# A convolution tile held ahead of a layer norm, gate columns moved behind it, ones products in the next norm's wait, and four more weights' low parts by VectorE

## Chip, cores and metric

One core of a Trainium2 chip runs the whole kernel. The metric is the device time of one execution in microseconds (us), as the median of several runs. "The profile" is one execution recorded by the hardware profiler, with its page and its trace.

## What is computed

A decoder trunk of two layers over 1024 tokens (S) of 1024 channels (D), float32 in and out. Cut to what matters:

```python
for i in range(2):
    mod = silu(c) @ ada_w[i] + ada_b[i]            # six vectors of D per layer
    sh_m, sc_m, g_m, sh_f, sc_f, g_f = split(mod, 6)
    h = rms_norm(x, norm_mix_g[i]) * (1 + sc_m) + sh_m
    if i == 0:                                     # convolution mixer
        a, g = split(h @ w1 + b1, 2)
        u = a * sigmoid(g)
        u = causal_depthwise_conv(u, w_dw, 31 taps) + b_dw
        y = silu(layer_norm(u)) @ w2 + b2
    else:                                          # pooling mixer, windows 2, 4, 8, 16
        y = grouped(trailing_mean(h) - h) @ w_grp * ls
    x = x + (1 + g_m) * y
    h = rms_norm(x, norm_ffn_g[i]) * (1 + sc_f) + sh_f
    x = x + (1 + g_f) * ((silu(h @ w_gate) * (h @ w_up)) @ w_down)   # inner width 2816
out = rms_norm(x, final_g)
```

The vector g_f of layer 0 is the "output gate" of the title: modulation j = 5, first used where the first feed-forward block's down products are added to x.

## The kernel before

**Layout.** Channels lie on the 128 partitions, in KT = 8 tiles of 128; tokens lie along the free dimension, in two halves, A (tokens 0 to 511) and B (512 to 1023). The halves go through the same stages one after the other, so that one half's products can stand in PE's queue while the other half's elementwise work is done. A is ahead of B.

**Weights in two parts.** A product in full float32 is made of three fast ones: high part of the weight with high part of the activation, high with low, low with high. So a product of one 128-channel tile of weights is 3 x 8 = 24 instructions ("24 products"). A weight of 128x1024 arrives in a `raw` buffer by a DMA that SP issues; ACT copies the rounded high part into a `w` tile; the low part comes in one of two ways. Either ACT writes the negated high-order copy of raw and POOL issues a DMA that reads the weight a second time and adds it (`load_weight(summed=True)`, line 413), or DVE subtracts (`low=V_`; a unit marked `own` takes this way, lines 546 and 564). There are nine `w` tiles (`W_BUFS`), so a weight's loading waits for products that free the tiles of an earlier one.

**Order.** PE's order is written by hand: `unit(...)` appends a piece of work to a list, and `run_units` emits them one after another, with the weights that they take loaded ahead. `need(name)` puts all that is left of a task there. Tasks are generators of elementwise work (norms, taps of the convolution, layer norm); `pace` steps them between PE's units by a planner's clock of what each engine has been given. A task that yields a word waits until a planned time: those in `LOAD` are counted from PE's clock, "stats" from the work given to DVE and ACT. The order on the other engines is then a scheduler's.

**The stage of the change** (layer 0, convolution):

- `conv_in((B, p))` makes the 24 + 24 products of a and g for B's tile p. A's layer norm (`layer_norm_silu`, task `ln_a`) needs A's eight tiles of convolved u; its sum `acc` is spread over the partitions by `mean`, a product with ones, and the variance by `var` and `rstd`. `rest` is B's tiles 0 to 4. With `HOLD = 1` the last of them (p = 4, the "held tile") is emitted behind the output products `y` of A (`conv_out(A)`); `HOLD_LN` is the number of tiles that stand just ahead of `need("ln_a")`. The steps of `ln_a` on PE (`mean`, `var`, `rstd`) fall among the tiles' products where the planner's clock puts them.
- `ada_columns` works out modulations j = 2 to 5 of layer 0 on PE, as products of columns of `ccols` with rows of the weight (`ada<-adaw`), two weights to a group; two buffers (`ADA_BUFS`) hold the weights, which SP loads. `columns_done` spreads the result (`adac`), and DVE adds the bias. All four modulations are done before `y` of A, but for the spread of the last, which stands behind `y`'s first three outputs.
- The norm that follows `conv_out(A)` (`norm`, task `norm_a`, through `mean_rsqrt`) takes the sum of squares of x (`var`), a root on DVE (`col`), its spreading (`rstd`), and gives the eight tiles of h as `hhi` and `hlo` to the feed-forward's `gate` and `up` products. `need("norm_a")` ends it.
- Behind it start the modulation of layer 1 (`ada_task(1, ...)`, dots on DVE), B's taps and B's layer norm, beside A's feed-forward. `conv_out(B)` stands `OUT_B = 3` units before that block's end.
- From B's feed-forward of layer 0 on, `ffn_mixed` emits a block: plain pairs, then pairs made with fewer products out of sums of quarters, and `rest`, the plain units from f = 16 to 21, in which one unit (`rest[4]`) has its weights' low parts by DVE and the other units of down products `dn` (`ffn_p2`) theirs by POOL's DMAs.

`warm(count)` emits products of ones with ones, whose result nobody reads (tile `idle`); before, it is used only at the kernel's start.

Of the kernel before, what the change touches and what calls it, by code (L numbers as in the profile page):

```python
# [39 lines left out]
HOLD = 1  # L40
FIRST = 4
SHARED = (5, 6)
HOLD_LN = 0
# [6 lines left out]
LOAD = {"load": 6.0, "late": 15.0, "settle": 8.0, "slow": 18.0, "next": 4.0}  # L50
# [63 lines left out]
def trunk(ctx, tc, xT, c, vec, ada, adan, w1, w2, wgu, wdn, wpl, wph, out):  # L114
# [94 lines left out]
    class Task:  # L209
# [6 lines left out]
        def step(self, e):  # L216
            if e != "V" or self.done or clock["PE"] < self.until and not forced[0]:
                return False
            try:
                if self.mark is None:  # L220
                    self.mark = clock["PE"] - V_.spent
                said = next(self.gen)
                if said == "wait":
                    return False
                if said in LOAD:
                    self.until = clock["PE"] + LOAD[said]
                elif said is not None:
                    self.until = (self.mark + V_.spent if self.urgent else max(clock["V"], clock["S"])) + (DELAY if self.urgent or not lax[0] else DELAY_BEHIND)[said]
                    self.mark = None
            except StopIteration:  # L230
                self.done = True
                tasks.remove(self)
            return True
# [206 lines left out]
    def mean_rsqrt(acc, n, keep=False, tag="col1"):  # L440

        count = n // P
        yield "stats"
        b = bank("var")
        for i in range(count):
            matmul(b[:, i : i + 1], acc[:, i * P : (i + 1) * P], ones[:, 0:1], start=True, stop=True)
        v, t = b[:, :count], b[:, 16 : 16 + count]  # L450
        V_.tensor_scalar(v, v, EPS, None, op0=ADD)
        col = tmp.tile([P, 16], F32, tag=tag, name=nm("col"), bufs=1)[:, :count]
        yield from rsqrt(v, col, t)
        yield "spread"
        r = spare_bank("rstd") if "taps_done" in st else bank("rstd")
        for i in range(count):
            matmul(r[:, i * P : (i + 1) * P], col[:, i : i + 1].broadcast_to([P, P]), ident, start=True, stop=True)
        r = r[:, :n]
        if not keep:
            return r  # L460
        held = temp(n, "ny", 2)
        S_.copy(held, r)
        return held
# [58 lines left out]
    def norm(ch, l, ffn, key, keep=False, squares=None):  # L522
        h = [(slot(ch, "hhi"), slot(ch, "hlo")) for _ in range(KT)]
        st[key] = h
        if squares is not None:
            rstd = yield from mean_rsqrt(squares.acc, ch.n, keep)
# [261 lines left out]
    def layer_norm_silu(ch):  # L788
# [9 lines left out]
        yield "stats"  # L798
# [26 lines left out]
    def conv_out(ch, squares, then=None):  # L825
# [20 lines left out]
        for ds in [(0, 1, 2), *((d,) for d in range(3, KT))]:  # L846
# [343 lines left out]
    def ffn_mixed(ch, l, until, at_end=False):  # L1190
# [25 lines left out]
        if not at_end:  # L1216
            rest[4] = own(rest[4])
# [76 lines left out]
    idle = spare_bank("idle")  # L1294

    def warm(count):
        for _ in range(count):
            matmul(idle[:, :P], ones, ones, start=True, stop=True)

# [140 lines left out]
    def ada_first(take):  # L1440
        T["ada", 0] = Task(ada_columns((2, 3, 4, 5)), False, 0)
        T["ada", 0].free = True
# [27 lines left out]
    conv_out(A, sq_a, lambda take: [now(columns_done(*g, bank("adac"))) for g in held_back])  # L1470
    unit(lambda take: T.__setitem__("norm_a", Task(norm(A, 0, True, ("h", 0), squares=sq_a), True)))
    for p in rest[len(rest) - HOLD :]:
        conv_in((B, p))
    need("norm_a")
    unit(lambda take: stretch.__setitem__(0, STRETCH))


    unit(lambda take: T.__setitem__(("ada", 1), ada_task(1, range(6))))
# [3 lines left out]
    for i, (e, ws) in enumerate(fa):  # L1482
        if i == len(fa) - OUT_B:
# [3 lines left out]
            unit(lambda take: T.__setitem__("norm_bf", Task(norm(B, 0, True, ("h", 1), squares=sq_b), True)))  # L1487
        unit(e, *ws)
    need("norm_bf")
# [122 lines left out]
```

## Time and profile before

| what | value |
|---|---|
| median of three runs | 1824.46 us |
| the three runs | 1816.51 to 1829.71 us |
| the profiled execution | 1815.78 us |
| its span in the trace | 1814.0 us |
| its mean granted TensorE clock | 0.993 |
| PE busy | 1774.6 us, 98% |
| DVE / ACT / POOL busy | 1317.4 / 1028.3 / 568.6 us |
| DMA | 335.39 MB, mean 185 GB/s |

The span is what the trace covers from first to last instruction; the execution's own time is 1.8 us more. A row of a timeline gives the start, the time of the row's instructions together, engine, line, operation, out<-in by the program's tile names, shapes and count, and in brackets the idle time ahead of it with what ended it. A float32 product that is not in the fast form leaves two records: four `ada` instructions are x8, ten `idle` are x20.

### The profile page before, as it was taken

To read this page: it belongs to the slowest core of one execution; us is meant where nothing else is said; L and a number is where in the kernel's file an instruction comes from. 1 tells how busy PE (TensorE), PEld (TensorE's weight loads), DVE (VectorE), ACT (ScalarE), POOL (GpSimd) and SP (SyncE) were. 2 spreads that over 40 slices of the span, in tenths; PEclk is the share of its full clock that TensorE was granted. 3 is DMA by queue.
4 is the path that set the end of the run, shared out by engine and by line. 5 is a ranking of instruction groups with operands and counts; after the bars stand their busy time and mean duration, and the time that the engine had idled before them with its cause. 6 is when DMAs were issued, how large, how long until landed. Compare 5 with 4: busy or idle time off the path is not lost.

```text
span 1814.0 us, 26209 instructions
## 1 busy us (share of the span) xinstructions
PE 1774.6 (98%) x9748; PEld 1518.4 (84%) x9748; DVE 1317.4 (73%) x2133; ACT 1028.3 (57%) x1597; POOL 568.6 (31%) x620
## 2 busy tenths in 40 slices
PE   9999899999999999999999999999999999999997
PEld 7777677888888788899998878999987889999986
DVE  8689846988774228889978468787694578887745
ACT  4776667767656455555554456555544546555543
POOL 0389724877833112111117122111161211011111
PEclk9999999999999999999999999999999999999998
DMA  9868767888978887867766877545558866655462
GB/s 308 278 183 258 190 165 192 223 219 227 233 190 219 231 217 192 242 198 209 205 155 144 203 165 184 142 130 136 134 139 196 185 138 169 180 140 140 125 142 70
DMA packets 113937, 335.39 MB, mean 185 GB/s; under 512 B 11281, under 2 KB 21649, under 8 KB 113810
## 3 DMA queue, kind: packets, MB, share of 16 engines
q1 hardware_dynamic: 76656, 222.56, 36.5%
q0 software_dynamic: 36000, 110.12, 34.0%
q8 instruction: 76, 1.25, 0.3%
q10 hardware_dynamic: 1154, 1.05, 0.2%
q14 instruction: 51, 0.42, 0.1%
HBM read 329.49 MB, written 4.19 MB: 184 GB/s over the span
## 4 chain that ended last, share of the span: by engine, by line
PE 83%; DMA 4%; DVE 4%; issue 4%; POOL 3%; ACT 2%; POOLq 0%; SPq 0%; DVEq 0%; ACTq 0%
PE dn L130 23%; PE gate L130 23%; PE up L130 22%; PE y L130 4%; PE a L130 3%; PE first L130 2%; DMA w<-in_wdn_dram 2%; PE g L130 2%; DMA adaw<-in_adan_dram 1%; ACT w L108 1%; POOL pa L108 1%; DMA w<-in_w_dram 1%; PE ada L130 1%; POOL w L413 1%; DVE t L108 1%
## 5 line engine op out<-in xcount | busy, mean ns | idle before, releaser
L130 PE MATMUL dn<-ghi,w 128*128 128x512 f32 (+1 forms) x1440 | 469.6, 389 | 5.7 <-DMA w<-in_wdn_dram 5.2
L108 ACT CAST w<-raw 128x1024 fp32r<-128x1024 f32 (+1 forms) x390 | 319.8, 823 | 154.6 <-PE dn L130 66.9
L108 ACT ACTIVATE w<-raw 128x1024 fp32r<-128x1024 f32 (+1 forms) x250 | 230.4, 921 | 304.0 <-PE dn L130 100.7
L108 DVE SCALAR_TENSOR_TENSOR x<-dn,gains,x 128x512 f32<-128x512 f32 (+1 forms) x360 | 263.1, 736 | 86.1 <-PE dn L130 82.9
L130 PEld LDWEIGHTS dn<-ghi,w 128*128 128x128 f32 x1440 | 269.1, 189 | 59.8 <-DMA w<-in_wdn_dram 7.0
L130 PE MATMUL gate<-hhi,w 128*128 128x512 f32 (+1 forms) x1088 | 310.3, 358 | 0.0
L130 PE MATMUL up<-hhi,w 128*128 128x512 f32 (+1 forms) x1088 | 310.1, 358 | 0.0
L130 PE MATMUL dn<-glo,w 128*128 128x512 f32 (+1 forms) x720 | 279.4, 388 | 0.1
L108 POOL TENSOR_TENSOR pa<-pa,pr 128x512 f32<-128x512 f32 x170 | 234.8, 1489 | 23.1 <-ACT pr L108 20.5
L1064 POOL DMA_DIRECT2D w<-in_wgu_dram x80 | 69.7, 871 | 499.4 <-PE up L130 147.5
L130 PEld LDWEIGHTS gate<-hhi,w 128*128 128x128 f32 x1088 | 196.7, 189 | 30.9
L130 PEld LDWEIGHTS up<-hhi,w 128*128 128x128 f32 x1088 | 196.6, 189 | 30.5
L130 PE MATMUL gate<-hlo,w 128*128 128x512 f32 (+1 forms) x544 | 195.0, 358 | 1.4 <-DVE hlo L108 1.4
L130 PE MATMUL up<-hlo,w 128*128 128x512 f32 (+1 forms) x544 | 194.6, 358 | 0.0
L413 POOL DMA_DIRECT2D w<-in_wgu_dram x92 | 82.2, 893 | 312.8 <-ACT w L108 289.1
L108 DVE SCALAR_TENSOR_TENSOR ca<-u,vecs,ca 128x512 f32<-128x512 f32 x250 | 174.0, 750 | 0.9
L108 DVE TENSOR_TENSOR t<-t,up 128x512 f32<-128x512 f32 (+1 forms) x88 | 54.9, 625 | 154.7 <-PE up L130 134.6
L130 PEld LDWEIGHTS dn<-glo,w 128*128 128x128 f32 x720 | 136.1, 189 | 23.3 <-POOL glo L108 0.5
L108 DVE TENSOR_TENSOR w<-raw,w 128x512 fp32r<-128x512 f32 (+1 forms) x140 | 107.7, 775 | 33.0 <-ACT w L108 29.7
L108 ACT ACTIVATE pr<-u,vecs 128x512 f32<-128x512 f32 x170 | 115.3, 717 | 24.1 <-POOL pa L108 16.9
L130 PEld LDWEIGHTS gate<-hlo,w 128*128 128x128 f32 x544 | 102.6, 189 | 17.9 <-DVE hlo L108 2.3
L130 PEld LDWEIGHTS up<-hlo,w 128*128 128x128 f32 x544 | 102.7, 189 | 15.5
(193 smaller groups left out, 3333.8 us busy)
## 6 DMA issues: line engine op xcount, KB each, us to landing
raw<-in_wgu_dram SPq DMA_DIRECT2D x176, 512.0 KB, 5.0
w<-in_wgu_dram POOLq DMA_DIRECT2D x92, 512.0 KB, 8.0
raw<-in_wdn_dram SPq DMA_DIRECT2D x88, 512.0 KB, 5.4
adaw<-in_ada_dram SPq DMA_DIRECT2D x64, 512.0 KB, 5.2
raw<-in_w_dram SPq DMA_DIRECT2D x42, 512.0 KB, 6.4
w<-in_wdn_dram POOLq DMA_DIRECT2D x42, 512.0 KB, 8.3
w<-in_wgu_dram POOLq DMA_DIRECT2D x80, 256.0 KB, 5.4
adaw<-in_adan_dram SPq DMA_DIRECT2D x32, 512.0 KB, 6.0
```

The source lines that it names most:

```text
L108: self.last = self.order(getattr(self.eng, name)(out, *args, **kw))
L130: last_mm[0] = nc.tensor.matmul(out, lhsT, rhs, start=start, stop=stop, **kw).ins.name
L413: order(nc.gpsimd.dma_start(as_src(lo), src, accum_op=ADD))
L1064: order(nc.gpsimd.dma_start(lo, src, accum_op=ADD))
```

## The change

It has five parts.

1. The held tile goes from behind `y` of A to ahead of it (`HOLD` 0, `HOLD_LN` 1). The layer norm's steps shift against the tiles: `mean` from behind tile 2 to the middle of tile 3, `var` and `rstd` from tile 3's g to tile 4's. A's `mean` is timed from PE's clock ("mean": 6.0) rather than from DVE's.
2. The output gate's columns (j = 5) are a generator of their own, `gates`. The spread of j = 4 stays behind the first unit of `conv_out(A)`, and there the generator issues its first two loads; its four groups of products come behind `conv_out(A)`, behind `need("norm_a")`, and behind the first two units of A's feed-forward; the spread and the start of layer 1's modulation come at unit `GROUP + 1` = 3.
3. `mean_rsqrt` of `norm_a` gets ten ones products behind `var` and ten behind `rstd`.
4. `conv_out(B)` begins with a unit of two outputs, not three.
5. In `ffn_mixed`, two units of down products (f = 16, 17 and f = 20, 21) get their weights' low parts by DVE: four weights in each of two blocks. Eight accumulating DMAs of POOL and eight negated copies of ACT go, eight subtractions of 128x1024 on DVE come.

The diff, without what repeats:

```diff
-HOLD = 1
+HOLD = 0
 FIRST = 4
 SHARED = (5, 6)
-HOLD_LN = 0
+HOLD_LN = 1
...
-LOAD = {"load": 6.0, "late": 15.0, "settle": 8.0, "slow": 18.0, "next": 4.0}
+LOAD = {"load": 6.0, "late": 15.0, "settle": 8.0, "mean": 6.0, "slow": 18.0, "next": 4.0}
...
                 if said in LOAD:
                     self.until = clock["PE"] + LOAD[said]
+                    if said == "mean":
+                        self.mark = None
...
+    def warm(count):
+        if count:
+            idle = spare_bank("idle")
+            for _ in range(count):
+                matmul(idle[:, :P], ones, ones, start=True, stop=True)
+
-    def mean_rsqrt(acc, n, keep=False, tag="col1"):
+    def mean_rsqrt(acc, n, keep=False, tag="col1", warmed=0):
...
             matmul(b[:, i : i + 1], acc[:, i * P : (i + 1) * P], ones[:, 0:1], start=True, stop=True)
+        warm(warmed)
         v, t = b[:, :count], b[:, 16 : 16 + count]
...
             matmul(r[:, i * P : (i + 1) * P], col[:, i : i + 1].broadcast_to([P, P]), ident, start=True, stop=True)
+        warm(warmed)
...
     def layer_norm_silu(ch):
...
-        yield "stats"
+        yield "stats" if ch.i else "mean"
         b = bank("mean")
...
     def conv_out(ch, squares, then=None):
...
-        for ds in [(0, 1, 2), *((d,) for d in range(3, KT))]:
+        n = 2 if ch.i else 3
+        for ds in [range(n), *((d,) for d in range(n, KT))]:
...
     def ffn_mixed(ch, l, until, at_end=False):
...
         if not at_end:
-            rest[4] = own(rest[4])
+            for i in (4, 5, -1):
+                rest[i] = own(rest[i])
...
     def ada_first(take):
-        T["ada", 0] = Task(ada_columns((2, 3, 4, 5)), False, 0)
+        T["ada", 0] = Task(ada_columns((2, 3, 4)), False, 0)
...
     sq_a = Squares(A)
-    conv_out(A, sq_a, lambda take: [now(columns_done(*g, bank("adac"))) for g in held_back])
-    unit(lambda take: T.__setitem__("norm_a", Task(norm(A, 0, True, ("h", 0), squares=sq_a), True)))
+    gates = ada_columns((5,))
+
+    def spread_held(take):
+        now(columns_done(*held_back.pop(), bank("adac")))
+
+    def gates_ahead(take):
+        spread_held(take)
+        next(gates)
+    conv_out(A, sq_a, gates_ahead)
+    unit(lambda take: next(gates))
+    unit(lambda take: T.__setitem__("norm_a", Task(norm(A, 0, True, ("h", 0), squares=sq_a, warmed=10), True)))
     for p in rest[len(rest) - HOLD :]:
         conv_in((B, p))
     need("norm_a")
+    unit(lambda take: next(gates))
     unit(lambda take: stretch.__setitem__(0, STRETCH))
-    unit(lambda take: T.__setitem__(("ada", 1), ada_task(1, range(6))))
     taps(B, *range(KT))
     put("ln_b", lambda: layer_norm_silu(B))
     fa = ffn(A, 0, False)
...
+        if i == GROUP + 1:
+            unit(spread_held)
+            unit(lambda take: T.__setitem__(("ada", 1), ada_task(1, range(6))))
         unit(e, *ws)
+        if i < GROUP:
+            unit(lambda take: next(gates, None))
```


**Order on PE at A's mean.** Before, g of B's tile 2 ends (`g_1990`), the mean follows, then a group of ada and a of tile 3 (`a_2126`):

```order
L130 MATMUL g_1990<-hhi_777,w_1834 128x512
L130 MATMUL g_1990<-hlo_778,w_1834 128x512
L130 MATMUL g_1990<-hhi_777,w_1835 128x512
L130 MATMUL mean_2064<-acc_1622,ones 128x512
L130 MATMUL ada_2003<-adaw_2014,ccols 32x256 x4
L130 MATMUL ada_2003<-adaw_2016,ccols 32x256 x4
L130 MATMUL a_2126<-hhi_763,w_1954 128x512
L130 MATMUL a_2126<-hlo_764,w_1954 128x512
L130 MATMUL a_2126<-hhi_763,w_1955 128x512
```

With the change, tile 2's products are followed by a of tile 3 (`a_2059`), then the mean and g of tile 3 (`g_2060`):

```order
L130 MATMUL a_2059<-hlo_778,w_1952 128x512
L130 MATMUL a_2059<-hhi_777,w_1953 128x512
L130 MATMUL a_2059<-hhi_779,w_1952 128x512
L130 MATMUL a_2059<-hlo_780,w_1952 128x512
L130 MATMUL a_2059<-hhi_779,w_1953 128x512
L130 MATMUL mean_2092<-acc_1624,ones 128x512
L130 MATMUL g_2060<-hhi_765,w_1980 128x512
L130 MATMUL g_2060<-hlo_766,w_1980 128x512
L130 MATMUL g_2060<-hhi_765,w_1981 128x512
```

Tile 3's 24 products of a moved from behind the mean to ahead of it, and the ada groups behind it are gone.

**Order on PE behind the output products of A.** Before, the last `y` is followed by a of the held tile:

```order
L130 MATMUL y_2573<-vhi_2234,w_2454 128x512
L130 MATMUL y_2573<-vlo_2235,w_2454 128x512
L130 MATMUL y_2573<-vhi_2234,w_2455 128x512
L130 MATMUL a_2629<-hhi_763,w_2492 128x512
L130 MATMUL a_2629<-hlo_764,w_2492 128x512
L130 MATMUL a_2629<-hhi_763,w_2493 128x512
```

and 24 rows further by the norm's `var`, with g of the held tile behind it:

```order
L130 MATMUL a_2629<-hhi_777,w_2492 128x512
L130 MATMUL a_2629<-hlo_778,w_2492 128x512
L130 MATMUL a_2629<-hhi_777,w_2493 128x512
L130 MATMUL var_2655<-ones,acc_2381 128x1 x4
L130 MATMUL g_2630<-hhi_763,w_2530 128x512
L130 MATMUL g_2630<-hlo_764,w_2530 128x512
L130 MATMUL g_2630<-hhi_763,w_2531 128x512
```

With the change, a group of ada stands behind `y`, then `var`, ones, `rstd`, ones, a group of ada and the feed-forward's gate products:

```order
L130 MATMUL y_2593<-vlo_2248,w_2474 128x512
L130 MATMUL y_2593<-vhi_2247,w_2475 128x512
L130 MATMUL ada_2631<-adaw_2423,ccols 32x256 x4
L130 MATMUL ada_2631<-adaw_2425,ccols 32x256 x4
L130 MATMUL var_2660<-ones,acc_2396 128x1 x4
L130 MATMUL idle_2665<-ones 128x128 x10
L130 MATMUL rstd_2689<-ident,col_2677 128x128 x4
L130 MATMUL idle_2694<-ones 128x128 x10
L130 MATMUL ada_2631<-adaw_2640,ccols 32x256 x4
L130 MATMUL ada_2631<-adaw_2642,ccols 32x256 x4
L130 MATMUL gate_2757<-hhi_2644,w_2512 128x512
L130 MATMUL gate_2757<-hlo_2645,w_2512 128x512
```

Forty-eight products of the held tile left this place; two groups of ada and twenty ones products came.

**The down group's low parts in layer 0, B, beside the pool mixer of A.** Before, POOL's row has two accumulating DMAs for them between the mixer's windows (`win`):

```order
L108 TENSOR_TENSOR win_9148<-win_9148,recip 128x15
L108 TENSOR_TENSOR win_9177<-win_9176 128x524
L108 TENSOR_TENSOR win_9148<-win_9148,hp_8876 128x15
L108 TENSOR_TENSOR win_9177<-win_9176 128x512
L413 DMA w_9261<-in_wdn_dram 128x1024
L108 TENSOR_TENSOR win_9177<-win_9177,recip 128x15
L108 TENSOR_TENSOR win_9177<-win_9177,hp_8877 128x15
L413 DMA w_9270<-in_wdn_dram 128x1024
L413 DMA w_9332<-in_wpl_dram 128x1024
L413 DMA w_9339<-in_wpl_dram 128x1024
```

With the change, DVE's row has the subtractions (`w_9294`, `w_9302`) between the same mixer's steps:

```order
L108 TENSOR_TENSOR mxlo_9169<-win_9144,mxhi_9168 128x512
L108 SCALAR_TENSOR_TENSOR win_9189<-win_9189,hp_8909 128x497
L108 TENSOR_TENSOR w_9294<-raw_9291,w_9293 128x1024
L108 CAST mxhi_9205<-win_9189 128x512
L108 TENSOR_TENSOR mxlo_9206<-win_9189,mxhi_9205 128x512
L108 TENSOR_TENSOR win_9247<-win_9248 128x520
L108 TENSOR_TENSOR w_9302<-raw_9299,w_9301 128x1024
L108 SCALAR_TENSOR_TENSOR win_9248<-win_9248,hp_8910 128x497
L108 TENSOR_TENSOR t_9286<-t_9286,up_9215 128x512
L108 CAST mxhi_9256<-win_9248 128x512
```

The two low parts left POOL's queue and stand between DVE's steps of the mixer (`mxhi`, `mxlo`).

More of the change, by code (lines that the diff above doesn't have):

```diff
@@ L520, in modulated, with norm @@
         V_.scalar_tensor_tensor(lo, t, sh, hi.bitcast(F32), op0=ADD, op1=SUB)
-    def norm(ch, l, ffn, key, keep=False, squares=None):
+    def norm(ch, l, ffn, key, keep=False, squares=None, warmed=0):
         h = [(slot(ch, "hhi"), slot(ch, "hlo")) for _ in range(KT)]
@@ L525, in norm @@
         if squares is not None:
-            rstd = yield from mean_rsqrt(squares.acc, ch.n, keep)
+            rstd = yield from mean_rsqrt(squares.acc, ch.n, keep, warmed=warmed)
         else:
@@ L1293, in trunk @@
         matmul(spread_c[h], ones[0:1, :], crow[:, h * 512 : h * 512 + 512], start=True, stop=True)
[L1294 to L1298, printed above, removed]
     acc = temp(A.n, "acc", 2)
```

## The prediction

> **What bounds the kernel now.** The page's first part says that TensorE is busy almost throughout, so only its gaps and its clock can be won. The waits of PE, largest first, name them:
>
> ```profile
> PE 1774.6 (98%) x9748; PEld 1518.4 (84%) x9748; DVE 1317.4 (73%) x2133; ACT 1028.3 (57%) x1597; POOL 568.6 (31%) x620
> PE mean L130 <- DVE mod L108: 7.0, 1, 7.0
> PE dn L130 <- DMA w<-in_wdn_dram: 5.2, 4, 1.9
> PE ada L130 <- DMA adaw<-in_adan_dram: 4.2, 3, 2.6
> PE y L130 <- DMA w<-in_w_dram: 2.2, 3, 1.3
> ```
>
> Columns: who waits for what, us in total, times, longest. These four are 18.6 us, 1.0% of the run, and the edits touch the order at each. The busy time per stretch has the granted clock third from the end of a row:
>
> ```profile
> 207.00:215.00 8.00, 0.98 (x3) 0.50 (x2) 5.42 (x9) 2.49 (x4) 4.40 (x6) 0.74 0.90 183
> 215.00:232.00 17.00, 17.00 (x98) 11.79 (x96) 10.56 (x25) 10.37 (x15) 4.08 (x4) 0.92 0.53 149
> 232.00:238.00 6.00, 3.23 (x20) 1.24 (x19) 3.01 (x5) 2.63 (x5) 0.87 (x1) 0.73 0.95 257
> 1366.00:1379.00 13.00, 12.22 (x46) 9.87 (x47) 6.29 (x9) 1.38 (x3) 0.00 (x0) 0.87 0.53 129
> ```
>
> Behind a gap of some 2 us the clock falls as well, and that costs about as much as a short gap: 6.0 x (1 - 0.73) = 1.6 us at 232, 13.0 x (1 - 0.87) = 1.7 at 1366.
>
> **The mean of A's layer norm.** Between PE's last `pz`, which ends at 194.29, and the mean stand two runs of 24 products today (a and g of B's tile 2) with a group of ada between; with the change it is three runs of 24 (a and g of tile 2, then a of tile 3) and no ada: the held tile, 4, takes the later place beside `var` and `rstd` that tile 3 had. The first two rows below are of the timeline and of the chain of work that ended last, the next two of that chain, the last of the timeline:
>
> ```profile
> 194.29 0.50 PE L130 MATMUL a<-hhi,w 128*128 128x512 f32 x1
> 282.90 5.44 PE a L130 x24
> 209.85 1.30 POOL pa L108
> 213.49 0.69 DVE acc L108
> 214.33 2.05 PE L130 MATMUL mean<-acc,ones 128*128 128x512 f32 x2 [7.02 <-DVE mod L108]
> ```
>
> PE would reach the mean at 194.29 + 3 x 5.44 = 210.6. The sum that it reads ends at 213.49 + 0.69 = 214.18, behind a chain of POOL's adds for the last tap and two DVE adds, whose places on their engines the change leaves as they are. The wait is then 214.2 - 210.6 = 3.6 instead of 7.02: **-3.4**. POOL's and DVE's rows in that stretch get one instruction more or less of 0.7 to 1.3, so I leave the chain 2 us on either side: -5.4 to -1.4. The clock falls behind 3.6 as it does behind 7.0, I take; were it not to, 17.0 x (1 - 0.92) = 1.4 more would be won.
>
> **The ada columns of the output gate.** Their loads are waited for today at the end of the layer norm's stretch:
>
> ```profile
> 227.48 8.50 DMA adaw<-in_adan_dram
> 234.78 1.08 PE L130 MATMUL ada<-adaw,ccols 128*32 128x256 f32 x8 [2.62 <-DMA adaw<-in_adan_dram]
> 236.02 1.08 PE L130 MATMUL ada<-adaw,ccols 128*32 128x256 f32 x8 [0.16 <-DMA adaw<-in_adan_dram]
> ```
>
> The groups leave this place, so 2.62 + 0.16 = **-2.8**, and the lower clock behind it, worked out above, **-1.6**. What is late next here is `y`'s first activation. Its low part ends with the row
>
> ```profile
> 234.29 0.69 DVE L108 TENSOR_TENSOR vlo<-t,vhi 128x512 fp32r<-128x512 f32 x1
> ```
>
> at 234.98. PE, done with `rstd` at 234.78 - 2.62 = 232.16, has 12 products of the held tile's g first (half of 5.44), so it comes to `y` at 234.9 and to the low part one product later: just in time. Four groups leave and four return behind the output products and the first feed-forward units; busy time is the same, net 0. The first pair that returns has its loads far ahead in SP's queue. The second pair's wait for the two buffers, which the first group frees at T + 1.07 (T: the end of `y`), and stand behind one weight load on SP: issued at about T + 2, landed by the 8.50 of the row above at T + 10.5. They are wanted at T + 3.65 + 0.95 + 2.48 + 1.05 + 2.48 = T + 10.6 (the norm's steps, next part). I take no wait; the price if that cover goes is a rival below.
>
> **The norm that follows.** Today 24 and then 12 products of the held tile hide the squares' sum behind `y`. They are gone from there, and a group of ada and 2 x 10 ones products stand instead.
>
> ```profile
> 282.71 1.06 ACT L108 ACTIVATE w<-raw 128x1024 fp32r<-128x1024 f32 x1 [2.34 <-PE y L130]
> 285.85 0.69 DVE L108 TENSOR_TENSOR acc<-acc,t 128x512 f32<-128x512 f32 x1 [0.72 <-ACT t L108]
> 288.18 0.95 PE L130 MATMUL var<-ones,acc 128*128 128x1 f32 x8
> 291.39 0.16 DVE L108 SCALAR_TENSOR_TENSOR col<-var,col 128x4 f32<-128x4 f32 x1
> 291.80 1.05 PE L130 MATMUL rstd<-ident,col 128*128 128x128 f32 x8
> 292.89 2.72 DVE L108 SCALAR_TENSOR_TENSOR t<-x,gains,rstd 128x512 f32<-128x512 f32 x4 [1.34 <-PE rstd L130]
> 295.53 1.41 DVE L108 SCALAR_TENSOR_TENSOR hlo<-t,mod,hhi 128x512 fp32r<-128x512 f32 x2
> 296.33 0.50 PE L130 MATMUL gate<-hlo,w 128*128 128x512 f32 x1 [0.52 <-DVE hlo L108]
> 307.10 0.50 PE L130 MATMUL gate<-hlo,w 128*128 128x512 f32 x1 [0.91 <-DVE hlo L108]
> 13.50 2.48 PE L130 MATMUL idle<-ones 128*128 128x128 f32 x20
> ```
>
> `y` ends at 282.90, where the row of 24 `a` quoted above begins; the sum of squares at 285.85 + 0.69 = 286.54, some 3.65 later, behind a weight's copy on ACT, the bias, the residual add and the last square. One group of ada lies in it (half the 2.16 us of the two rows of eight above, taken at the full clock: 1.07), so `var` waits **+2.6**. Behind it in PE's order stand ones, `rstd`, ones, ada and all gate products: nothing overtakes. As behind the 2.62 at 234.78, the clock falls: **+1.6**. The ones products are 10 instructions (20 records) in 2.48, twice: **+5.0**. What they cover: the root on DVE ends at 291.55, 2.4 after `var`'s end (288.18 + 0.95), so the first ten fill that wait to 0.1; the first tile's low part comes about 3.4 after `rstd`, and ten ones and an ada group are 2.48 + 1.07 = 3.55. That is more than the 2.72 + 0.1 of products that stood there, so the gate's two waits, 0.52 + 0.91, go: **-1.4**; the second is for the last tile's low part, ahead of which fewer of the taps' instructions stand on DVE now. Two smaller waits arise in A's `y`: the layer norm's third tile stands on ACT behind a copy that now waits for the held tile's g and the third weight's low comes later. No row shows either. Bounds for both together are nothing (both are hidden by the 72 products ahead) and 1.3, the largest wait of `y` for a weight in the first fence; I take **+0.9**, an estimate nearer to that row, since two of them meet.
>
> Conv stage: -3.4 - 2.8 - 1.6 - 1.4 + 2.6 + 1.6 + 5.0 + 0.9 = **+0.9**. The tile moves one wait away and makes another.
>
> **Output products of B, two outputs first.** Three weights are wanted at once today; with two the third's arrival is not waited for:
>
> ```profile
> 631.00 0.73 PE L130 MATMUL y<-vhi,w 128*128 128x512 f32 x2 [1.27 <-DMA w<-in_w_dram]
> 652.03 0.74 PE L130 MATMUL y<-vhi,w 128*128 128x512 f32 x2 [0.34 <-DMA w<-in_w_dram]
> ```
>
> 1.27 + 0.34 = **-1.6** (at worst one of the two stays).
>
> **Lows of two down groups by DVE.** Eight accumulating DMAs of POOL and eight negated copies of ACT go; eight subtractions of DVE come.
>
> ```profile
> 990.89 7.60 DMA w<-in_wdn_dram
> 998.54 10.13 PE dn L130 x43
> 1355.28 11.45 DMA w<-in_wdn_dram
> 1366.78 11.75 PE dn L130 x43
> 983.62 1.64 DVE L108 TENSOR_TENSOR w<-raw,w 128x1024 fp32r<-128x1024 f32 x1
> 991.02 0.69 DVE L108 TENSOR_TENSOR mxlo<-win,mxhi 128x512 fp32r<-128x512 f32 x1
> 1008.67 1.39 PE y L130 x6
> ```
>
> A DMA of 7.60 to 11.45 ends each of the four waits; a subtraction takes 1.64. So all 5.2 go: **-5.2**, and the run of 43 products goes from 11.75 to 10.13: **-1.6**. Two subtractions in DVE's row delay the pool mixer by 3.3; its last part ends at 991.71, and its reader starts at 1008.67, 17 us later, so it hides. If it did not, the price would be those 3.3 at each of two places.
>
> **Sum:** +0.9 - 1.6 - 5.2 - 1.6 = **-7.5** on the profiled execution, 1815.8, so 1808.3. That execution lies below the median of 1824.46 and near the shortest run; with the same distance the median is 1824.46 - 7.5 = **1817.0**.
>
> **Rivals.** (1) *The clock holds in the norm's wait*, since 2.6 us of idle would be too short to lower it. For it: the row
>
> ```profile
> 134.19 0.64 PE L130 MATMUL ada<-adaw,ccols 128*32 128x256 f32 x8 [1.47 <-DMA adaw<-in_adan_dram]
> ```
>
> is followed by products at full pace. Against: the 2.62 at 234.78, and the 1.94 of PE's waits that stands ahead of the row of 1366. Then the +1.6 falls away: -9.1, 1815.4. The Trainium skill ("TensorE: Matmul & The Clock Gate", "HAM oscillation — how this bites in real kernels") asks that no idle gap of TensorE be over about 3.4 us; by that rule the gap of 2.6 costs no clock and the time is this rival's. The trace disagrees: 0.73 behind a gap of 2.62.
>
> (2) *Ada products are late.* For it: a load can take the 11.45 of the down row when the queues are full; then the second pair lands at T + 13.5, 2.9 after it is wanted, and the clock adds 1.1. Result -7.5 + 4.0 = -3.5, 1821.0. Against: the 8.50 row just fits.
>
> (3) *The lows by DVE come no earlier.* The raw rows come by the same queues; if the raw and not the low is last, the 5.2 and 1.6 stay: -0.7, 1823.8. Against: the four waits name the accumulating DMA, asked for only when both copies are done.
>
> (4) *Slower: B's layer norm becomes late.* The mean of B stands 12 products of a down group (half of 5.44) earlier in PE's order now, 2.7 us, and the modulation of layer 1, whose dots share DVE with B's taps, begins later, nearer to the sum.
>
> ```profile
> 516.73 3.85 DVE L108 TENSOR_TENSOR acc<-acc,u 128x512 f32<-128x512 f32 x4
> 529.48 1.02 PE L130 MATMUL mean<-acc,ones 128*128 128x512 f32 x2
> ```
>
> Today the sum is ready at 520.58, 8.9 ahead. It decides from a delay of 8.9 - 2.7 = 6.2 us; from 13.7 it eats the 7.5, and at 20 the kernel is 20 - 13.7 = 6.3 slower: 1830.8. Against: the work of DVE ahead of that point is the same in number.
>
> **How the numbers follow.** Forecast 0.60, rival 1 0.12, rival 2 0.13, rival 3 0.09, rival 4 0.06. The lowest ends together (-2.0 on the mean, -1.4 of its clock, -1.6 of rival 1) make -7.5 - 5.0 = -12.5, 1812; the three runs before lie up to 8 below their median, so the low end is 1804. Above, rival 3's 1823.8 and a shift of some 3 give 1827; rival 4 is left out. A measurement of this kernel tells about 1%, 18 us, from no change. Faster by more needs the low ends and a lucky draw: 0.10; slower by more needs rival 4 at over 25 us: 0.04; within: 0.86.
>
> **What would show it.** A wait of about 3.6 at A's mean and about 2.6 at A's next `var`, the latter with a low clock behind it; no waits on `adan`; `idle` in two rows of 2.5; no wait of `dn` on `in_wdn` in two of the three mixed stages; PE's busy time up by some 5. Wrong would be: a mean that waits 7 still (the chain moved with PE), an ada wait in the feed-forward's first units, or B's mean waiting at all.

## The result, and the profile after

| | before | changed |
|---|---|---|
| median of ten runs, us | 1822.93 | 1810.40 |
| range, us | 1814.26 to 1829.71 | 1807.99 to 1812.60 |
| ratio of the times, 95% interval | | 0.9936 [0.9918, 0.9954] |
| span of the profiled run, us | 1814.0 | 1809.0 |

The changed kernel is 0.64% faster, and the interval lies wholly below 1. Two things can't be read from the pair of profiles: the profiled spans differ by only 5.0 us where the medians differ by 12.5, and the runs of before lie 15 us apart, those of the changed kernel 5.

First the busy time and the waits of PE in the changed kernel:

```profile
PE 1777.5 (98%) x9788; PEld 1525.3 (84%) x9788; DVE 1323.8 (73%) x2139; ACT 1022.9 (57%) x1593; POOL 569.1 (31%) x614
...
PE rstd L130 <- DVE col L108: 7.3, 5, 2.7
PE var L130 <- DVE acc L108: 6.5, 3, 4.5
PE mean L130 <- DVE acc L108: 3.7, 1, 3.7
...
PE y L130 <- DMA w<-in_w_dram: 1.8, 1, 1.8
```

Of the four rows of before, the 5.2 for `in_wdn` is gone, the 4.2 for `in_adan` is 0.3, `mean` is 3.7 instead of 7.0. A new one has come: `var` waits 4.5 at one place. The timeline of PE shows that place and the next rows, with POOL and DVE beside it:

```profile
212.90 2.04 PE L130 MATMUL mean<-acc,ones 128*128 128x512 f32 x2 [3.71 <-DVE acc L108]
...
287.27 1.87 PE L130 MATMUL var<-ones,acc 128*128 128x1 f32 x8 [4.51 <-DVE acc L108]
289.01 4.62 PE L130 MATMUL idle<-ones 128*128 128x128 f32 x20
293.41 1.27 PE L130 MATMUL rstd<-ident,col 128*128 128x128 f32 x8
294.52 2.40 PE L130 MATMUL idle<-ones 128*128 128x128 f32 x20
...
283.24 2.60 DVE L108 SCALAR_TENSOR_TENSOR x<-t,gains,x 128x512 f32<-128x512 f32 x1 [3.28 <-ACT t L108]
...
283.61 1.68 POOL L108 TENSOR_SCALAR pa<-u,vecs 128x512 f32<-128x512 f32 x2
```

The first ten ones products took 4.62 us, the second ten 2.40: the first ran at half clock. The residual add on DVE took 2.60 us where every other of its kind near it takes 0.75, and two steps of POOL for B's taps lie in the same time. The granted clock (third from the end) says when it fell:

```profile
283.00:287.20 4.20, 0.00 (x0) 0.00 (x0) 3.27 (x2) 1.76 (x3) 2.26 (x3) 0.98 0.97 237
287.20:290.00 2.80, 2.73 (x12) 2.73 (x13) 0.70 (x6) 0.00 (x0) 0.00 (x0) 0.50 1.00 288
290.00:294.00 4.00, 4.00 (x21) 4.00 (x21) 1.32 (x8) 0.00 (x0) 0.00 (x0) 0.52 0.51 129
294.00:300.00 6.00, 6.00 (x52) 4.77 (x51) 5.20 (x8) 2.70 (x4) 0.00 (x0) 1.00 0.23 63
```

It falls as the wait ends and stays at one half for nearly 7 us (287.0 to 293.9), and products that only keep PE busy are slowed with the rest.

### The profile page after: what moved, and what is told of

It reads as the page before. It is cut to its first block, busy times and chain, and to the rows that moved or that the text cites. A ratio compares the mean times of both kernels' runs of the same rounds, so it can differ in the third digit from the quotient of the medians.

```text
span 1809.0 us, 26287 instructions
## 1 busy us (share of the span) xinstructions
PE 1777.5 (98%) x9788; PEld 1525.3 (84%) x9788; DVE 1323.8 (73%) x2139; ACT 1022.9 (57%) x1593; POOL 569.1 (31%) x614
## 3 DMA queue, kind: packets, MB, share of 16 engines
q10 hardware_dynamic: 1154, 1.05, 0.2%
## 4 chain that ended last, share of the span: by engine, by line
PE 92%; DVE 2%; issue 2%; DMA 2%; ACT 1%; POOL 1%; POOLq 0%; SPq 0%; ACTq 0%; DVEq 0%
PE dn L130 26%; PE gate L130 25%; PE up L130 25%; PE y L130 5%; PE a L130 3%; PE g L130 2%; PE first L130 2%; PE ada L130 1%; PE idle L130 1%; ACT w L108 1%; PE rstd L130 1%; ACT t L108 0%; DMA adaw<-in_adan_dram 0%; PE var L130 0%; DMA w<-in_w_dram 0%
## 5 line engine op out<-in xcount | busy, mean ns | idle before, releaser
L108 ACT ACTIVATE w<-raw 128x1024 fp32r<-128x1024 f32 (+1 forms) x242 | 222.0, 917 | 267.1 <-PE dn L130 82.1
L108 POOL TENSOR_TENSOR pa<-pa,pr 128x512 f32<-128x512 f32 x174 | 241.4, 1488 | 41.4 <-ACT pr L108 38.3
L108 DVE TENSOR_TENSOR w<-raw,w 128x512 fp32r<-128x512 f32 (+1 forms) x148 | 117.8, 802 | 34.3 <-ACT w L108 31.3
L130 PEld LDWEIGHTS up<-hlo,w 128*128 128x128 f32 x544 | 102.6, 189 | 15.5
```

Of the source, the lines that this page charges most:

```text
L108: self.last = self.order(getattr(self.eng, name)(out, *args, **kw))
L130: last_mm[0] = nc.tensor.matmul(out, lhsT, rhs, start=start, stop=stop, **kw).ins.name
```

## The experiments

Times are compared with runs of the kernel before on the same chip. The medians of before were 1822.04 in the first group of four, 1819.38 in the second, 1820.89 in the third; beside the changed kernel it was 1822.93. So a difference of medians to the changed kernel carries up to 3.5 us of difference between the groups, and where the two disagree the ratios are the safer comparison. Beside the times, the profiles are cut into stages by the starts and ends of PE's products:

| stage (PE) | three outputs, lows by POOL | the same stage with the part changed |
|---|---|---|
| first to last `y` of B | 45.9, 52.3, 49.3, 53.2 | 43.7 in all ten profiles with two outputs |
| `y` of B to the pool mixer's `y` of A | 334.8, 336.9, 335.7, 337.3 | 333.0 to 333.1 in all ten with lows by DVE |
| from there to the pool mixer's `y` of B | 358.8, 357.3, 357.6, 357.2 | 353.7 to 353.8 |
| from there to PE's last product | 417.5, 418.0, 420.3, 421.1 | 416.2 to 417.8 |
| last `pz` to first `y` of B, held tile behind `y`, gate's columns ahead | 433.4, 434.7, 435.8, 437.4, 433.8 | 438.9, 436.7, 437.3 with parts 1 to 3 |

(The first number of each row is the first profile of before.)

### The low parts alone, and all but the low parts

The part alone, on the kernel before:

```diff
         if not at_end:
-            rest[4] = own(rest[4])
+            for i in (4, 5, -1):
+                rest[i] = own(rest[i])
```

> The kernel before with the fifth part alone: both more groups of down products get their weights' low parts by DVE. Theory A (the lows carry most of the gain, and the kernel before varies from run to run because its accumulating DMAs land at varying times): 9 to 12 us under the kernel before, about 1811 to 1814, and its runs lie within some 5 us of each other. Theory B (the lows give what the one profile showed, 5.2 of waits and 1.6 of clock, and the variation is in the convolution stage): 5 to 7 us under the kernel before, about 1816 to 1818, and the runs still lie some 15 us apart. In both, no wait of dn on in_wdn at the places near 998, 1078, 1366 and 1447 us.

Measured: 1813.03 us median (1808.90 to 1814.03), ratio 0.9938 [0.9917, 0.9959]. That is 9.0 us under the median of before, with runs 5.1 us apart.

The same edit undone, on the changed kernel:

```diff
         if not at_end:
-            for i in (4, 5, -1):
-                rest[i] = own(rest[i])
+            rest[4] = own(rest[4])
```

> The changed kernel with the fifth part undone: these weights' low parts by POOL's accumulating DMAs again. Theory A: 9 to 12 us slower than the changed kernel, about 1820, with runs some 15 us apart. Theory B: about 5 to 7 us slower than the changed kernel, 1815 to 1817, with runs within 5 us. Its profile shows waits of dn on in_wdn again, 5 us or more.

Measured: 1818.60 us (1813.33 to 1823.92), ratio 0.9979 [0.9964, 0.9995]; 8.2 us over the changed kernel, with runs 10.6 apart. Its four waits are there again, in the row of PE's waits and in the timeline:

```profile
PE dn L130 <- DMA w<-in_wdn_dram: 7.3, 4, 2.3
...
999.45 0.73 PE L130 MATMUL dn<-ghi,w 128*128 128x512 f32 x2 [2.30 <-DMA w<-in_wdn_dram]
1078.98 0.76 PE L130 MATMUL dn<-ghi,w 128*128 128x512 f32 x2 [0.96 <-DMA w<-in_wdn_dram]
1368.12 0.73 PE L130 MATMUL dn<-ghi,w 128*128 128x512 f32 x2 [2.14 <-DMA w<-in_wdn_dram]
1448.54 1.02 PE L130 MATMUL dn<-ghi,w 128*128 128x512 f32 x2 [1.90 <-DMA w<-in_wdn_dram]
```

Alone, the part agrees with theory A in size, and nearly in spread, though six runs say less of a spread than the 23 of before. Undone, it lies between the theories, nearer to A. By the ratios the part is worth 11.3 us alone and 7.8 on the changed kernel. The stage table gives the same: means of 336.2, 357.7 and 419.2 us without, 333.1, 353.7 and 417.1 with, together 9.3 us. The first profile of before had 0.93 at the fourth place where this one has 1.90. The clock fell behind that 1.90, and not behind the 2.30 and the 2.14.

### The kernel before once more

> The kernel before once more, for a second profile of it: ratio 1.000 within 0.002. If the profiled execution is a typical one (1820 or more), theory A wants its waits of dn on in_wdn and their clock at 12 us or more where the first profile had 6.8; theory B wants the added time ahead of 320 us.

Measured: ratio 0.9996 [0.9982, 1.001], 1822.84 us median. This profile is of a typical run (span 1821.2), 7.2 us longer than the first one. It is longer at a place that neither theory named, the output products of B (the last row but one is the first profile of before, behind its first wait):

```profile
632.32 0.73 PE L130 MATMUL y<-vhi,w 128*128 128x512 f32 x2 [2.72 <-DMA w<-in_w_dram]
656.64 0.92 PE L130 MATMUL y<-vhi,w 128*128 128x512 f32 x2 [2.00 <-DMA w<-in_w_dram]
...
633.00:640.00 7.00, 7.00 (x26) 5.55 (x25) 0.00 (x0) 0.00 (x0) 0.00 (x0) 0.76 0.50 135
657.00:665.00 8.00, 8.00 (x30) 6.41 (x29) 1.35 (x2) 3.46 (x5) 1.06 (x2) 0.79 1.05 271
...
631.00:638.00 7.00, 7.00 (x31) 5.80 (x32) 1.17 (x3) 0.00 (x0) 0.00 (x0) 1.00 0.75 195
...
PE dn L130 <- DMA w<-in_wdn_dram: 5.6, 4, 2.0
```

The same two waits were 1.27 and 0.34 in the first profile, with the clock at 1.00 behind them; here they are 2.72 and 2.00, and the clock falls to 0.76 and 0.79 behind them, so the stage takes 52.3 instead of 45.9. The waits for `in_wdn` are 5.6, near the 5.2 of the first profile. So theory A's 12 us are not there, and neither is theory B's added time ahead of 320 us.

### Two outputs first, undone and alone

On the changed kernel:

```diff
-        n = 2 if ch.i else 3
+        n = 3
```

> The changed kernel with the fourth part undone: the output products of B begin with three outputs. Theory G (the forecast's size): two waits of y on in_w of 1.27 and 0.34, so 1.6 us slower than the changed kernel. Theory H (the profiled execution of before was a lucky one at this place: the second profile has 2.72 and 1.99 there and takes 6.2 us longer for the stage): 4 to 8 us slower, 1814 to 1818, and runs further apart than 5 us.

Measured: 1817.79 us (1815.98 to 1823.28), ratio 0.9991 [0.9977, 1.0004]. The two waits in its profile:

```profile
639.98 0.73 PE L130 MATMUL y<-vhi,w 128*128 128x512 f32 x2 [3.68 <-DMA w<-in_w_dram]
664.27 0.73 PE L130 MATMUL y<-vhi,w 128*128 128x512 f32 x2 [1.99 <-DMA w<-in_w_dram]
```

And on the kernel before:

```diff
-        for ds in [(0, 1, 2), *((d,) for d in range(3, KT))]:
+        n = 2 if ch.i else 3
+        for ds in [range(n), *((d,) for d in range(n, KT))]:
```

> The kernel before with the fourth part alone: B's output products begin with two outputs. The stage from the first to the last of these products took 45.9 and 52.3 us in two profiles of before, and 43.7 with the change. Theory H: 4 to 7 us under the kernel before, and the stage within 1 us of 43.7. Theory G: 1.6 us under it.

Measured: 1816.19 us (1814.84 to 1821.97), ratio 0.9976 [0.9963, 0.9988], 4.7 us under before by the medians; the stage took 43.7. Theory H holds in both. The four profiles with three outputs have a mean of 50.2 for the stage, so by these four draws this small edit is worth some 6.5 us of PE's time, not 1.6.

### What the first three parts bring together

The kernel before with both edits, that of the low parts and that of the two outputs:

```diff
-            rest[4] = own(rest[4])
+            for i in (4, 5, -1):
+                rest[i] = own(rest[i])
...
-        for ds in [(0, 1, 2), *((d,) for d in range(3, KT))]:
+        n = 2 if ch.i else 3
+        for ds in [range(n), *((d,) for d in range(n, KT))]:
```

> The kernel before with the fourth and fifth parts; the changed kernel without its first three, that is. Theory M (the first three parts cost more than they bring: the stage sums of the profiles give up to 2.6 us more until the first gate product): 1 to 3 us faster than the changed kernel, 1807.5 to 1809.5. Theory N (they bring 1 to 3 us, the waits for the gate's columns being gone): 1811.5 to 1813.5.

Measured: 1807.01 us (1806.87 to 1808.76), ratio 0.9927 [0.9914, 0.9939]. The median is 3.4 us under the changed kernel's. The two ratios' intervals overlap and the two kernels ran beside different runs of before, so by the times alone a cost is likely and not proven; a gain of 1 to 3 us (theory N) is not to be seen. The stage from `pz` to the first `y` of B has a mean of 435.0 in five profiles without the three parts and 437.6 in three with them, 2.6 more. Theory M has the sign, and its 1807.5 is missed by 0.5. The waits that the three parts aim at are all in this kernel: 6.6 for the mean, 3.5 for the gate's columns.

Cut finer, the same eight profiles show what the three parts gain and what they cost, with no overlap in any row but that of `y`:

| stage (PE), us | five without the three parts | three with them |
|---|---|---|
| last `pz` to A's mean | 20.0 to 20.1 | 20.2 |
| A's mean to first `y` of A | 22.7 to 23.2 | 20.5 to 21.9 |
| first to last `y` of A | 45.8 to 49.6 | 46.5 to 47.0 |
| from there to the first gate product | 12.5 | 15.5 to 16.1 |
| from there to the first `y` of B | 332.3 to 332.4 | 333.7 to 333.8 |

By the means the layer norm gains 1.9, and the norm behind `y` and the feed-forward cost 3.4 and 1.4.

### Without the ones products

```diff
-    unit(lambda take: T.__setitem__("norm_a", Task(norm(A, 0, True, ("h", 0), squares=sq_a, warmed=10), True)))
+    unit(lambda take: T.__setitem__("norm_a", Task(norm(A, 0, True, ("h", 0), squares=sq_a), True)))
```

> The changed kernel without the 2 x 10 ones products of A's norm; nothing else is left out. By the changed kernel's trace the first ten ran at half clock and took 4.62 us where the root takes 2.4, so without them rstd starts some 1.8 us earlier; the second ten only fill the wait for the first tile. Theory C (the ones only fill, and the clock is already lost): 1 to 3 us faster than the changed kernel, about 1808. Theory D (they keep the clock): two waits of 2.4 and about 1.3 us more with PE idle, and half clock behind them for longer, 1 to 3 us slower than the changed kernel, about 1812.5.

Measured: 1809.78 us (1808.52 to 1811.86), ratio 0.9925 [0.9907, 0.9943]; by the medians 0.6 under the changed kernel, which the times can't tell from nothing. In the profile:

```profile
286.70 1.86 PE L130 MATMUL var<-ones,acc 128*128 128x1 f32 x8 [4.51 <-DVE acc L108]
291.14 2.05 PE L130 MATMUL rstd<-ident,col 128*128 128x128 f32 x8 [2.57 <-DVE col L108]
296.74 0.50 PE L130 MATMUL gate<-hlo,w 128*128 128x512 f32 x1 [1.04 <-DVE hlo L108]
```

`rstd` starts 4.4 us behind `var` instead of 6.1. From the end of `y` to the first gate product it is 13.8 us instead of 16.1, and 1.3 of these 2.3 come back until B's `y`. Theory C is right on the place and the sign of the profile, and the times don't show its 1 to 3 us: behind `var` the ones come too late to keep the clock, and run past the root. They are not without effect, though. Without them the clock stays at one half for 10.2 us where it was nearly 7:

```profile
285.24:295.48 10.24, 6.21 (x33) 4.45 (x33) 4.90 (x18) 2.03 (x4) 0.00 (x0) 0.50 0.61 163
```

### The tile back behind the output products, without ones

```diff
-HOLD = 0
+HOLD = 1
-HOLD_LN = 1
+HOLD_LN = 0
...
-    unit(lambda take: T.__setitem__("norm_a", Task(norm(A, 0, True, ("h", 0), squares=sq_a, warmed=10), True)))
+    unit(lambda take: T.__setitem__("norm_a", Task(norm(A, 0, True, ("h", 0), squares=sq_a), True)))
```

> The changed kernel with the first and third parts undone: the held tile behind A's output products again, no ones products in A's norm; the gate's columns, the two outputs first and the lows stay as in the change, and the layer norm's mean stays timed from PE's clock. Theory E (the tile only trades one exposed chain for another): the norm's section gets 16.1 - 14.7 = 1.4 us shorter beside the tile's own 10.9, the layer norm's section loses the tile's 10.9 and gains waits of about 2.1, 2.4 and 2.7 and 2.5 of clock; together 2 to 3 us faster than the changed kernel, about 1808, as without the ones. Theory F (the norm's wait with the lost clock is much the dearer one): 5 us faster or more, under 1806.

Measured: 1810.69 us (1810.00 to 1811.50), ratio 0.9948 [0.9932, 0.9963], so no faster than the changed kernel. Without the tile the layer norm waits three times:

```profile
224.96 1.02 PE L130 MATMUL var<-ones,acc 128*128 128x1 f32 x8 [3.45 <-DVE acc L108]
228.56 2.05 PE L130 MATMUL rstd<-ident,col 128*128 128x128 f32 x8 [2.57 <-DVE col L108]
232.75 0.80 PE L130 MATMUL y<-vhi,w 128*128 128x512 f32 x1 [2.15 <-DVE vhi L108]
```

The tile covers one chain or the other, as theory E says; its 2 to 3 us were not there, for a reason that is left open, and theory F is excluded.

### B's first taps held back

```diff
                     G_.tensor_scalar(self.part, u[:, j : j + n], w(j), 0.0, op0=MUL, op1=ADD)
+                    if ch.i and "spread_a" in st:
+                        tc.add_manual_dep(G_.last.ins, st["spread_a"], mybir.DependencyInfo(mybir.DependencyClass.Sync, mybir.DependencyReason.DATA), reason="behind the root's spreading")
```

`spread_a` is the name of the last product behind `rstd` in A's norm.

> The changed kernel, with the first step of B's taps on POOL made to wait for the spreading of A's root (a wait on PE's rstd). Theory I (POOL's two steps at 283.61 slow DVE's residual add at 283.24 from 0.75 to 2.60 us): that add takes 0.75 again, var waits 2.6 instead of 4.51, and the kernel is about 1.9 us faster, 1808.5. Theory J (the add was slow for another reason, the weights' DMAs for instance): 2.6 us again and the time of the changed kernel.

Measured: 1808.09 us (1806.44 to 1812.62), ratio 0.9937 [0.9919, 0.9955]; the times don't tell it from the changed kernel, the profile does:

```profile
284.37 0.75 DVE L108 SCALAR_TENSOR_TENSOR x<-t,gains,x 128x512 f32<-128x512 f32 x1 [3.28 <-ACT t L108]
...
296.23 1.78 POOL L108 TENSOR_SCALAR pa<-u,vecs 128x512 f32<-128x512 f32 x2 [11.20 <-PE idle L130]
...
286.58 1.87 PE L130 MATMUL var<-ones,acc 128*128 128x1 f32 x8 [2.68 <-DVE acc L108]
```

With POOL's two steps elsewhere the add is 0.75 again, and `var` waits 2.68, which is the forecast's 2.6. Theory I holds. The kernel of the section above agrees without any holding: its steps on POOL begin at 291.41, and its add takes 0.75.

```profile
284.33 0.75 DVE L108 SCALAR_TENSOR_TENSOR x<-t,gains,x 128x512 f32<-128x512 f32 x1 [3.28 <-ACT t L108]
```

In all fourteen profiles this add takes 2.60 where the two steps lie beside it (six) and 0.75 where they don't (eight). The clock behind the shorter wait falls all the same:

```profile
287.00:290.00 3.00, 3.00 (x15) 3.00 (x16) 1.27 (x8) 0.00 (x0) 0.00 (x0) 0.50 0.95 258
```

### Ones ahead of the wait's end, and ahead of the mean

```diff
         yield "stats"
+        warm(2 * warmed)
         b = bank("var")
```

> The changed kernel with twenty more ones products, ahead of A's var, in the wait of 4.51 us (20 take 4.9 at most at full clock). Theory K (PE idle is what lowers the clock): no idle time is left ahead of var, the granted clock stays at 1.00 from 283 to 300 us where it was 0.84 and 0.78, the ten ones behind var take 2.4 instead of 4.62, and the kernel is about 3 us faster, 1807.5. Theory L (these ones products don't hold the clock, or delay var): no change, or up to 1 us slower.

Measured: 1806.17 us (1805.32 to 1807.80), ratio 0.9925 [0.9907, 0.9942]; 4.2 us under the changed kernel by the medians and 2.0 by the ratios, whose intervals overlap. What decides is the profile, with PE's timeline and the clock:

```profile
281.02 4.73 PE L130 MATMUL idle<-ones 128*128 128x128 f32 x40
285.61 1.05 PE L130 MATMUL var<-ones,acc 128*128 128x1 f32 x8
286.52 2.48 PE L130 MATMUL idle<-ones 128*128 128x128 f32 x20
289.23 1.13 PE L130 MATMUL rstd<-ident,col 128*128 128x128 f32 x8 [0.23 <-DVE col L108]
...
284.00:288.00 4.00, 4.00 (x37) 3.95 (x36) 1.96 (x9) 0.63 (x1) 0.00 (x0) 1.00 0.92 253
288.00:292.00 4.00, 3.77 (x34) 3.61 (x34) 2.44 (x9) 0.74 (x2) 0.00 (x0) 1.00 0.61 140
```

`var` still comes when its sum does, but the clock holds at 1.00, and the ten ones behind it take 2.48 and end with the root. From `y`'s end to the first gate product it is 13.4 instead of 16.1 us: theory K.

The same idea in the layer norm, with the products' time left out of the planner's clock, so that the order stays:

```diff
         yield "stats" if ch.i else "mean"
+        if ch.i == 0:
+            planned = clock["PE"]
+            warm(14)
+            clock["PE"] = planned
         b = bank("mean")
```

> The changed kernel with fourteen ones products ahead of A's mean, in its wait of 3.7 us (some 3.5 us at full clock). By theory K the clock holds: mean takes 1.0 instead of 2.04, the 19 us behind it run at 1.00 instead of 0.93 (1.3 us), together 2.3 us faster than the changed kernel, about 1808. By theory L: no change.

Measured: 1806.93 us (1803.61 to 1808.78), ratio 0.9922 [0.9910, 0.9935].

```profile
209.53 3.29 PE L130 MATMUL idle<-ones 128*128 128x128 f32 x28
213.42 1.10 PE L130 MATMUL mean<-acc,ones 128*128 128x512 f32 x2 [0.61 <-DVE acc L108]
...
216.00:235.00 19.00, 19.00 (x92) 15.59 (x91) 14.00 (x31) 14.70 (x21) 4.88 (x6) 1.00 0.60 127
```

`mean` takes 1.10 instead of 2.04, and from `mean` to `y` it is 19.1 us instead of 21.9 (20.5 to 21.9 in the six kernels with this order and without these ones). `mean` starts 20.3 us behind the last `pz`, as it did without them (20.2), so the gain is the clock's: theory K again.

### All three together

The three edits above in one, with eleven ones ahead of `var`.

> The changed kernel with three additions: B's first taps on POOL held behind the spreading of A's root, eleven ones products ahead of A's var, fourteen ahead of A's mean. If the three gains are separate: 2.3 for the mean, 4.4 for the norm as with the twenty ones, and up to 1.8 for the residual add, where the twenty ones had covered a longer wait than is left: 6 to 8 us faster than the changed kernel, 1802.5 to 1804.5. If they are one and the same clock: no better than the twenty ones alone, 1806.

Measured: 1803.95 us (1803.27 to 1804.37), ratio 0.9906 [0.9892, 0.9920]: 6.4 us under the changed kernel by the medians and 5.5 by the ratios, 16.9 under the before of its own group, the fastest of all, with its runs within 1.1 us. The gains are separate: from `mean` to `y` it is 19.1 us as with the ones ahead of the mean alone, and from `y`'s end to the first gate product 12.0, less than with the ones alone (13.4) or the taps held alone (14.2).

## Why the prediction was right, and where its terms were off

The forecast was -7.5 us, with 1817.0 within 1804 to 1827; it is -12.5, with 1810.4. The direction and the mechanism of the parts that carry the gain were right. The sizes were off, and not all to the same side: the convolution stage, with the norm in it, came out dearer than forecast, and both edits on weights brought more.

- **The mean: right.** Forecast a wait of 3.6 and a lower clock behind it; 3.71, and `mean` at 2.04.
- **The gate's columns: right.** The waits of 2.62 and 0.16 are gone; the columns that moved wait nowhere, so rival 2 did not come.
- **The norm: the term was mis-sized.** From `y`'s end the forecast's steps are 3.65 + 0.95 + 2.48 + 1.05 + 2.48 + 1.07 = 11.7 us, with 1.6 for the clock 13.3; measured 16.1. The residual add, which the two steps on POOL slowed, is 4.51 - 2.68 = 1.8 of the missing 2.8 (shown by holding them back). The clock covers the rest: from `var`'s start to `rstd`'s end it is 7.4 where the forecast's rows have 4.5, so 2.9 for 1.6. "The first ten fill that wait to 0.1" failed because they were priced at the full clock. With the wait filled from ahead and the steps on POOL held back, the forecast's 11.7 is nearly reached, 12.0 in the last kernel.
- **The conv stage, +0.9:** by the stage table +2.6, by the medians +3.4. Besides the norm, one wait of A's `y` for a weight was 1.77 in the profile, where the forecast had 0.9 for two small ones; in the other profiles it is between nothing and 1.85, in the kernel before too, so no run shows that the change makes it.
- **Two outputs first, -1.6: the term that was furthest off.** "1.27 + 0.34" was read from one execution, in which these waits were short and the clock stayed up. Four profiles have 45.9 to 53.2 for the stage; two outputs make it 43.7 every time, 6.5 less than their mean.
- **The lows by DVE, -6.8:** right in mechanism and place; -9.3 by the stages, -9.0 and -8.2 by the medians. The subtractions delayed nothing that PE waits for, and rivals 3 and 4 did not come: no wait for `in_wdn`, none at B's mean. (Rival 3 has the raw rows come "by the same queues"; SP issues them, and POOL the accumulating DMAs.)

Sum by the stages: +2.6 - 6.5 - 9.3 = -13.2, beside -12.5 by the medians. The step that hid this is "with the same distance the median is": the profiled execution of before was 7 us under its own median because it was lucky in the waits that the change removes (4.3 us in the output products of B, some 2 in the three stages of the lows, against the means), and the changed kernel has them no more. For the pair of profiles, on which the -7.5 was worked out, the change is 5.0 us: -1.7 ahead of the last `pz`, +5.6 from there to B's first `y`, -2.2 in B's output products, -6.7 in the three stages of the lows. So the forecast promised 2.5 us more than its own profile gained and 5.0 less than the median did; that it lies between the two is luck.

Rival 1 did not come: the wait became 4.51 us, and the clock fell. With the wait cut to 2.68 it fell to one half too. That again disagrees with the rule of the Trainium skill ("TensorE: Matmul & The Clock Gate", "HAM oscillation — how this bites in real kernels") that rival 1 names, no idle gap over about 3.4 us. One such wait doesn't settle what another does, though: 2.30 us left the clock at 1.00 in the kernel with the low parts undone.

## What to carry to other kernels

- A profile is one draw: where a wait ends on a DMA its length is drawn anew in each run, and a second profile of the same kernel, from a typical run, would have shown the waits of B's `y` at 2.72 and 2.00 where the first had 1.27 and 0.34. The spread of the runs is the hint.
- Products that only keep the tensor engine busy belong ahead of the instruction that waits, where they fill the wait; behind it they run at the lowered clock and may outlast what they cover.
- An engine off the critical path can lengthen a single step on it: work that the scheduler pulls into an idle stretch of POOL may cost DVE there more than it gains (1.8 us here).

## What the runs showed of the hardware

- DVE's residual add of 128x512 took 2.60 us in six profiles, with two multiplications of 128x512 by a column on POOL beside it (1.68 together in the changed kernel), and 0.75 in the eight without them.
- Whether the clock falls behind a wait of some 2 us is not set by its length alone. In the second profile of before it fell to 0.72 behind 1.81 and held behind 2.04 (timeline of PE, then the stretches from the start of each wait, with the clock third from the end):

```profile
1005.18 1.22 PE L130 MATMUL dn<-ghi,w 128*128 128x512 f32 x2 [1.81 <-DMA w<-in_wdn_dram]
1375.13 0.74 PE L130 MATMUL dn<-ghi,w 128*128 128x512 f32 x2 [2.04 <-DMA w<-in_wdn_dram]
...
1003.00:1008.00 5.00, 3.19 (x9) 2.24 (x8) 1.35 (x2) 1.41 (x2) 0.88 (x1) 0.72 1.03 247
1373.00:1378.00 5.00, 2.96 (x13) 2.36 (x13) 2.10 (x3) 1.32 (x2) 0.86 (x1) 1.00 1.07 276
```

The traces say what parts the two. In each of the fourteen all changes of the granted clock, between 1.00 and 0.50, lie whole multiples of 3.413 us apart, to within 3 ns. Cut along these steps, from 10 to 1780 us of each trace, the clock fell at the end of 38 of the 39 steps that began at 1.00 and in which PE was idle for 1.79 us or more; of all the others, with less idle time, it fell behind three, each with the `var` near 75 us in it (four products of one column). So a wait of some 2 us lowers the clock when it lies whole in one step, like the 1.81, and not when a border parts it, like the 2.04 (0.74 and 1.31). The steps of the two waits, the first with the step behind it:

```profile
1001.77:1005.18 3.41, 1.60 (x7) 0.74 (x5) 0.69 (x1) 2.51 (x3) 0.88 (x1) 1.00 1.05 245
1005.18:1008.59 3.41, 3.40 (x8) 2.73 (x9) 1.36 (x3) 0.00 (x0) 0.00 (x0) 0.50 1.03 243
...
1370.41:1373.82 3.41, 2.67 (x12) 1.88 (x10) 0.69 (x1) 2.01 (x3) 0.55 (x1) 1.00 1.03 251
1373.82:1377.24 3.42, 2.11 (x9) 1.76 (x10) 1.53 (x3) 0.50 (x1) 0.31 (x1) 1.00 1.05 252
```

This is read from the traces; no run shifted a wait against the steps on purpose.

- Two drawn waits are left in these kernels: that of A's `y` for a weight, up to 1.85 us, and one of PE for the columns of modulation j = 3 near 133 us, nothing to 2.7. In the profiles where the latter is 2.5 and 2.7 (three outputs, taps held) the last `pz` ends at 197, in the others at 192.7 to 194.4, so it is worth up to 4 us of a run.
